# Modulation vectors of layer 1: one-row-per-condition matmuls replaced by weight-tile products on ACT, sums on GpSimd and one-column matmuls

## The chip, the cores and the metric

The kernel runs on 1 core of one Trainium2 chip. A core has five engines with a queue each, worked off in order: TensorE (PE, with its weight loads shown apart as PEld), VectorE (DVE), ScalarE (ACT), GpSimd (POOL) and SyncE (SP), which only issues transfers here. The metric is the device time of one execution in microseconds (us); the time shown is the median of three runs.

## What is computed

Two layers of a diffusion backbone over 512 latent tokens and 256 context tokens, model width 1024. Each layer's six modulation vectors (shift, scale and gate of the mixer, shift, scale and gate of the MLP) come from the condition `c`, and for the context from `c_ctx`:

```python
def adaln_modulation(cond, w_mod, b_mod):
    m = jax.nn.silu(cond) @ w_mod + b_mod          # w_mod: 1024 x 6144, one per layer
    return jnp.split(m[..., None, :], N_MOD, axis=-1)

for layer in range(DEPTH):                         # DEPTH = 2
    with_ctx_out = layer < DEPTH - 1
    sh1, sc1, g1, sh2, sc2, g2 = adaln_modulation(c, w_mod[layer], b_mod[layer])
    csh1, csc1, cg1, csh2, csc2, cg2 = adaln_modulation(c_ctx, w_mod[layer], b_mod[layer])
    h = rmsnorm(x, norm1_g[layer]) * (1.0 + sc1) + sh1
    h_c = rmsnorm(ctx, norm1_g[layer]) * (1.0 + csc1) + csh1
    mix, mix_c = hybrid_mixer(h, h_c, ...)         # S5 scan, gated DeltaNet, windowed attention, merge
    x = x + g1 * mix
    x = x + g2 * sq_relu_mlp(rmsnorm(x, norm2_g[layer]) * (1.0 + sc2) + sh2, w_ff1[layer], w_ff2[layer])
    if with_ctx_out:
        ...                                        # the same two updates of ctx, with cg1, csh2, csc2, cg2
return rmsnorm(x, final_norm_g)
```

In layer 1 the context has no output, so of its six vectors only `csh1` and `csc1` are used there: columns 0 to 2047 of the 6144.

## The kernel before

Everything is fp32. Features lie on the 128 partitions, tokens on the free axis; `x` is 128 x 8 x 768. A large product (`mm3`, L178) is three matmuls for each 128 x 128 weight tile: the weight and the activation are each split into a high part and a remainder, and high x high, high x low and low x high are added up in PSUM. `load_w` brings 128 x 1024 of weights (512 KB) over SP into `ws` (3 buffers), ACT writes the high part `wh` (L227), and the engine `g.wle` writes the remainder `wl` (L228): DVE in the MLP, GpSimd in most of the mixers. `wh` and `wl` have 2 buffers each, so ACT may start the split of a tile when PE has let go of the last but one.

The order of a run is: setup and modulation of layer 0, mixers, merge and MLP of layer 0, mixers, merge and MLP of layer 1. The change lies in the MLP of layer 0 (`mlp`, L1682 on). It works in four groups `gi`; each has eight up-projections (`up`, one weight tile column block `j` each, 24 matmuls of 512 columns and 24 of 256), relu and square, the split of the result (ACT `hh`, DVE `hl`), and then eight down-projections (`ff2`), whose results DVE adds to `x` (L1657). Between the up-projections, two background jobs that layer 1 needs are taken a step further, one step at a time:

- `adaln` (L241), the modulation of layer 1. One step is one block `nb` of 512 of the 6144 columns; there are 12, one after each odd `j`, so that the last comes in the third group. A step loads four tiles `wa` of 128 x 1024 (SP, 2 buffers), multiplies each half with the condition (`g.cs`, 32 columns of which two are used: row 0 is `c`, row 1 is `c_ctx`) as the stationary operand, eight fp32 matmuls of 512 columns, four of which stand side by side in the array's 32-column strips (L251); ACT copies the sums with a factor 0.5 (`ms`, L254), PE transposes them (L257), DVE adds the four strips (L259) and the bias (L261) into `g.modv`. Its two PSUM tiles come from the tag `s`, which has 2 buffers and serves the other background job too.
- `s5_tables` (L498 on), the tables of the S5 scan of layer 1. Sixteen steps, one after each `j`. Each is about fifty short DVE operations, transposes on PE (L558), small matmuls (L568) and DMAs of the results (L550, L561, L585). Its tiles `tX` and `tC` have one buffer each.

Layer 0's own modulation also uses `adaln`. A second call, `adaln(g, l + 1, ...)` in the MLP of layer 1, makes a generator that is never advanced. What layer 1 needs of `modv` is first read after the MLP (`norm_gain`, L275).

An engine's order is set when the program is built: the framework takes the instructions in program order as priority and simulates a timeline, and puts next on an engine what is ready in it. On the chip each engine then works off that fixed order and waits where a semaphore asks for it.

Of the kernel before, what the change touches and what calls it, by code (L numbers as in the profile page):

```python
# [8 lines left out]
F32 = mybir.dt.float32  # L9
# [3 lines left out]
OP = mybir.AluOpType  # L13
# [20 lines left out]
SM_G1, SM_G2, SM_GF, SM_BM, SM_CV, SM_DG, SM_SK, SM_AL, SM_DT, SM_D = 0, 16, 32, 40, 136, 256, 258, 274, 290, 306  # L34
# [120 lines left out]
def raw(t, off, dims):  # L155
    return bass.AP(tensor=t.tensor, offset=t.offset + off, ap=[list(t.ap[0])] + [list(x) for x in dims])
# [25 lines left out]
def setup(g):  # L182
    tc, nc, A = g.tc, g.nc, g.A
    es = g.es
    g.base = es.enter_context(tc.tile_pool(name="base", bufs=1))
    g.wp = es.enter_context(tc.tile_pool(name="wp", bufs=2))
    g.ps = es.enter_context(tc.tile_pool(name="ps", bufs=1, space=PSUM))
    g.dr = es.enter_context(tc.tile_pool(name="dr", bufs=1, space=DRAM))
    g.ca = g.base.tile([128, CA_N], F32, name="ca")
    nc.sync.dma_start(g.ca, A["ca"])  # L190
    g.sm = g.base.tile([128, SM_N], F32, name="sm")
    nc.sync.dma_start(g.sm, A["small"])
    g.ident = g.ca[:, CA_ID:CA_ID + 128]
    g.ones = g.base.tile([128, 32], F32, name="ones")
    nc.gpsimd.memset(g.ones, 1.0)
    g.cneg = g.base.tile([128, 1], F32, name="cneg")
    nc.gpsimd.memset(g.cneg, -0.5)
    g.cpos = g.base.tile([128, 1], F32, name="cpos")
    nc.gpsimd.memset(g.cpos, 0.5)
    g.hpi = g.base.tile([128, 1], F32, name="hpi")  # L200
    nc.gpsimd.memset(g.hpi, math.pi / 2)
    g.modv = g.base.tile([128, NL, 48, 2], F32, name="modv")
    g.g1 = g.base.tile([128, 8, 2], F32, name="g1a")
    g.g2 = g.base.tile([128, 8, 2], F32, name="g2a")

# [4 lines left out]
def pm(g, tag="m"):  # L210
    return g.ps.tile([128, 512], F32, name="p" + tag, tag=tag, bufs=PSB[tag])
# [9 lines left out]
def load_w(g, l, i, pool=None):  # L221
    nc = g.nc
    s = load_raw(g, g.A["wt"][l, i])
    pool, bufs = (g.wp, 2) if pool is None else (pool, 6)
    hi = pool.tile([128, 1024], F32R, name="wh", tag="wh", bufs=bufs)
    lo = pool.tile([128, 1024], F32R, name="wl", tag="wl", bufs=bufs)
    nc.scalar.copy(hi, s)  # L227
    g.wle.tensor_tensor(lo, s, hi.bitcast(F32), op=OP.subtract)  # L228
    return hi, lo
# [11 lines left out]
def adaln(g, l, nbs, pool, bufs=2):  # L241
    nc = g.nc
    for nb in nbs:
        ps = pm(g, "s")
        for kp in range(4):
            w = pool.tile([128, 1024], F32, name="wa", tag="wa", bufs=bufs)
            g.ad_last = nc.sync.dma_start(w, g.A["wmod"][l, nb, kp])
            for k2 in range(2):
                kt = kp * 2 + k2
                c = kt % 4  # L250
                nc.tensor.matmul(ps[32 * c:32 * c + 32, :], lhsT=g.cs[:, kt, :], rhs=w[:, k2 * 512:k2 * 512 + 512],  # L251
                                 start=kt < 4, stop=kt >= 4, tile_position=(0, 32 * c))
        ms = pool.tile([128, 512], F32, name="ms", tag="ms", bufs=1)
        nc.scalar.mul(ms, ps, 0.5)  # L254
        p2 = pm(g, "s")
        for j in range(4):
            nc.tensor.transpose(p2[:, j * 128:j * 128 + 128], ms[:, j * 128:j * 128 + 128], g.ident)  # L257
        md = pool.tile([128, 4, 2], F32, name="md", tag="md", bufs=1)
        nc.vector.tensor_reduce(md, raw(p2, 0, [[128, 4], [1, 2], [32, 4]]), axis=AX.X, op=OP.add)  # L259
        bm = g.sm[:, SM_BM + 48 * l + nb * 4:SM_BM + 48 * l + nb * 4 + 4]  # L260
        nc.vector.tensor_tensor(g.modv[:, l, nb * 4:nb * 4 + 4, :], md,  # L261
                                bm[:, :, None].to_broadcast([128, 4, 2]), op=OP.add)
        yield


def drain(it, n=1):
    for _ in range(n):
        next(it, None)
# [59 lines left out]
def passes(cx):  # L328
    return P_LC if cx else P_AB


def groups(cx):
    return [[p] for p in P_LC] if cx else [P_AB]
# [24 lines left out]
def gemm_x(g, w, grp, kts=range(8), src=None):  # L358
    ps = pm(g, "g")
    o = 0  # L360
    for p in grp:
        if src is None:
            hi, lo = g.hv[p.key]
            f = (lambda k: hi[:, k, :], lambda k: lo[:, k, :])
        else:
            f = (lambda k: src[k][0][:, p.sl], lambda k: src[k][1][:, p.sl])
        mm3(g, ps[:, o:o + p.n], w, list(kts), f)
        o += p.n
    return ps[:, :o], slice(grp[0].sl.start, grp[0].sl.start + o)
# [901 lines left out]
def split(g, hi, lo, src, scale):  # L1271
    g.nc.scalar.mul(hi, src, scale)
    g.nc.vector.scalar_tensor_tensor(lo, src, scale, hi.bitcast(F32), op0=OP.mult, op1=OP.subtract)
# [381 lines left out]
def ff2(g, l, w, m, p, hid):  # L1655
    acc, sl = gemm_x(g, w, [p], src=hid)
    g.nc.vector.scalar_tensor_tensor(g.x[:, m, sl], acc, g.modv[:, l, 40 + m, p.r:p.r + 1], g.x[:, m, sl],  # L1657
                                     op0=OP.mult, op1=OP.add)
# [23 lines left out]
def mlp(g, l, out):  # L1682
    nc, tc = g.nc, g.tc
    cx = l < NL - 1
    outs = ["l", "c"] if cx else ["l"]
    nn = TOK if cx else LAT
    if cx:
        tb = s5_tables(g, l + 1, lambda k, d: nc.vector, 1)
    with tc.tile_pool(name=f"ml{l}", bufs=1, reuse_waits="tile") as pool:
        ad = adaln(g, l + 1, range(12), pool)  # L1690
        def up(js, grps):
            ws = [load_w(g, l, W_F1 + j) for j in js]
            rs = [pool.tile([128, nn], F32, name="rl", tag="rl", bufs=2) for _ in js]
            for grp in grps:
                for w, r in zip(ws, rs):
                    acc, sl = gemm_x(g, w, grp)
                    nc.scalar.activation(r[:, sl], acc, AF.Relu)
            for r in rs:
                nc.vector.tensor_tensor(r, r, r, op=OP.mult)
                hh = pool.tile([128, nn], F32R, name="hh", tag="hh", bufs=9)  # L1700
                hl = pool.tile([128, nn], F32R, name="hl", tag="hl", bufs=9)
                split(g, hh, hl, r, 1.0)
                hid.append((hh, hl))

        for gi in range(4):
            hid = []
            for j in range(8):
                if gi > 0 or j > 1:
                    up([8 * gi + j], groups(cx))
                elif j == 0:  # L1710
                    up([0, 1], [[p] for p in passes(cx)])
                if cx:
                    drain(ad, j % 2)
                    drain(tb)
            last = gi == 3 and not cx
            if last:
                g.mp_.__exit__(None, None, None)
                last_group(g, l, pool, hid, out)
                break
            sts = [Stats(g, pool, p.n, 2, ("rl", nn), "ms") for p in P_LC] if cx and gi == 3 else None  # L1720
            ws = {}
            order = [(m, p) for m in range(8) for p in (P_LC if cx else P_LC[:1])]
            if sts:
                order = order[:12] + [(m, p) for p in P_LC for m in (6, 7)]
            for m, p in order:
                if m not in ws:
                    ws[m] = load_w(g, l, W_F2 + 8 * gi + m)
                ff2(g, l, ws[m], m, p, hid)
                if sts:
                    sts[P_LC.index(p)].add(m, g.x[:, m, p.sl])  # L1730
                    if m == 7:
                        st = sts[P_LC.index(p)]
                        g.pbs.append(st.bcast())
                        if PF and p.key == "l":
                            st.pace(PF)
                        else:
                            g.plan = []
    if cx:
        g.mp_.__exit__(None, None, None)
# [3 lines left out]
def hybrid_block(ctx, tc, A, out):  # L1743
# [3 lines left out]
    g.tb, g.hd, g.rside, g.pbs, g.plan, g.ldp, g.hst = {}, {}, "right", [], [], [], []  # L1747
    g.wle = nc.vector
    setup(g)
    s5a_open(g, 0)  # L1750
    cond_setup(g)
# [76 lines left out]
```

## Time and profile before

| | us |
|---|---|
| three runs | 2945.82, 2945.91, 2971.23 |
| median | 2945.91 |
| the profiled execution, its time | 2966.88 |
| the profiled execution, its span | 2965.1 |
| PE busy of the span | 2729.9 (92%) |
| DVE busy | 1669.2 (56%) |
| ACT busy | 908.1 (31%) |
| POOL busy | 558.1 (19%) |

Busy times are of the profiled execution. Matmuls overlap in the array, so PE's busy share is the share of time in which at least one runs, and the distance between the starts of two neighbours says what one costs. The MLP of layer 0 lies from about 1140 to 1765 us of the span. An fp32 matmul shows as two records (two LDWEIGHTS and two MATMUL), a transpose as one.

### The profile page before, as it was taken

The numbers are of one execution on the slowest core, as the hardware profiler recorded it, in microseconds if no ns is written. First come the engines' busy times: TensorE is split into PE (matmuls) and PEld (weight loads), VectorE is DVE, ScalarE is ACT, GpSimd is POOL, SyncE is SP. The second block draws the span as 40 slices with busy tenths as digits, with TensorE's granted clock in tenths as the row PEclk, the third lists the DMA queues.
The fourth block names the chain that finished last, engine by engine and source line by source line (L and its number), as shares of the span: only waits on it lengthen the run. The fifth ranks groups of instructions, "written<-read, shape, count | busy, mean of one in ns | idle before, by whom it ended". The sixth has DMA issues, their size and how long they took to land. (4 is left out here: it accounts for less than half of the span.)

```text
span 2965.1 us, 46215 instructions
## 1 busy us (share of the span) xinstructions
PE 2729.9 (92%) x17908; PEld 2193.9 (74%) x17908; DVE 1669.2 (56%) x4335; ACT 908.1 (31%) x1643; POOL 558.1 (19%) x733
## 2 busy tenths in 40 slices
PE   5698899999999999999999999758997999999998
PEld 1585578878677877787778878646775768789997
DVE  7839985245336647747432324997456368444443
ACT  2243344232222323223121324332342234323322
POOL 4643331030213300000000001442253133000000
PEclk8799899699999999999999999879997999999999
DMA  6564322236116433535341225223432226233231
GB/s 226 160 219 161 136 80 79 69 123 174 42 38 204 137 109 108 161 125 151 120 133 67 67 84 176 73 66 120 138 102 76 93 84 208 77 99 99 87 100 65
DMA packets 206620, 343.63 MB, mean 116 GB/s; under 512 B 89280, under 2 KB 121152, under 8 KB 206400
## 3 DMA queue, kind: packets, MB, share of 16 engines
q1 hardware_dynamic: 171712, 297.56, 31.4%
q0 software_dynamic: 9600, 36.71, 3.7%
q10 hardware_dynamic: 25088, 6.40, 1.0%
q8 instruction: 141, 2.31, 0.3%
q14 instruction: 79, 0.65, 0.1%
HBM read 269.04 MB, written 68.16 MB: 114 GB/s over the span
## 5 line engine op out<-in xcount | busy, mean ns | idle before, releaser
L228 DVE TENSOR_TENSOR wl<-ws,wh 128x1024 fp32r<-128x1024 f32 x234 | 293.5, 1256 | 341.0 <-ACT wh L227 306.8
L227 ACT CAST wh<-ws 128x1024 fp32r<-128x1024 f32 x272 | 284.8, 1049 | 606.4 <-PE pg L178 477.9
L178 PE MATMUL pg<-hhil,wh 128*128 128x512 f32 x720 | 296.4, 412 | 51.5 <-ACT cxp L867 35.9
L178 PE MATMUL pg<-hlol,wh 128*128 128x512 f32 x720 | 294.0, 409 | 0.4 <-DVE hlol L350 0.4
L178 PE MATMUL pg<-hhil,wl 128*128 128x512 f32 x720 | 293.1, 407 | 0.1
L178 PE MATMUL pg<-hh,wh 128*128 128x512 f32 (+1 forms) x832 | 285.6, 344 | 3.1 <-DVE x L1657 2.8
L178 PE MATMUL pg<-hlo,wh 128*128 128x512 f32 (+1 forms) x800 | 280.9, 351 | 6.2 <-DVE hlo L350 6.2
L178 PE MATMUL pg<-hhi,wh 128*128 128x512 f32 (+1 forms) x800 | 281.4, 352 | 5.1 <-ACT cxp L867 5.1
L178 PE MATMUL pg<-hh,wl 128*128 128x512 f32 (+1 forms) x832 | 284.0, 342 | 1.0 <-DVE wl L228 1.0
L178 PE MATMUL pg<-hl,wh 128*128 128x512 f32 (+1 forms) x832 | 284.7, 343 | 0.0
L178 PE MATMUL pg<-hhi,wl 128*128 128x512 f32 (+1 forms) x800 | 279.4, 349 | 0.0
L178 PEld LDWEIGHTS pg<-hhil,wh 128*128 128x128 f32 x720 | 139.5, 194 | 96.7 <-ACT cxp L867 37.4
L1657 DVE SCALAR_TENSOR_TENSOR x<-pg,modv,x 128x512 f32<-128x512 f32 (+1 forms) x104 | 64.9, 626 | 259.5 <-PE pg L178 259.3
L178 PEld LDWEIGHTS pg<-hlo,wh 128*128 128x128 f32 x800 | 154.7, 193 | 37.4 <-issue 14.0
L178 PEld LDWEIGHTS pg<-hh,wh 128*128 128x128 f32 x832 | 157.3, 189 | 33.8 <-issue 12.1
L178 PEld LDWEIGHTS pg<-hhi,wh 128*128 128x128 f32 x800 | 155.2, 194 | 31.6 <-issue 9.0
L178 PEld LDWEIGHTS pg<-hl,wh 128*128 128x128 f32 x832 | 157.4, 189 | 27.9 <-issue 10.6
L178 PEld LDWEIGHTS pg<-hhi,wl 128*128 128x128 f32 x800 | 154.6, 193 | 29.3 <-issue 11.7
L178 PEld LDWEIGHTS pg<-hh,wl 128*128 128x128 f32 x832 | 157.3, 189 | 22.8 <-issue 2.9
L178 PEld LDWEIGHTS pg<-hlol,wh 128*128 128x128 f32 x720 | 139.4, 194 | 36.8 <-issue 6.6
L178 PEld LDWEIGHTS pg<-hhil,wl 128*128 128x128 f32 x720 | 139.2, 193 | 36.9 <-issue 5.6
L307 POOL TENSOR_TENSOR nr<-nv,cneg 128x2 f32<-128x2 f32 (+1 forms) x10 | 9.3, 933 | 645.5 <-ACT nsq L290 350.2
(421 smaller groups left out, 6115.8 us busy)
## 6 DMA issues: line engine op xcount, KB each, us to landing
ws<-in_wt SPq DMA_DIRECT2D x272, 512.0 KB, 3.6
wa<-in_wmod SPq DMA_DIRECT2D x96, 512.0 KB, 4.3
gtd<-gr POOLq DMA_DIRECT2D x24, 384.0 KB, 2.9
tg<-gtd POOLq DMA_DIRECT2D x24, 384.0 KB, 3.5
tb<-tC SPq DMA_DIRECT2D x64, 128.0 KB, 2.3
cvd<-ctp SPq DMA_DIRECT2D x20, 384.0 KB, 2.6
gtd<-gr POOLq DMA_DIRECT2D x24, 256.0 KB, 2.6
tg<-gtd POOLq DMA_DIRECT2D x24, 256.0 KB, 3.1
```

Source lines behind the costliest of these rows:

```text
L178: g.nc.tensor.matmul(ps, lhsT=wt[:, a], rhs=x(k), start=i == 0, stop=i == n - 1)
L227: nc.scalar.copy(hi, s)
L228: g.wle.tensor_tensor(lo, s, hi.bitcast(F32), op=OP.subtract)
L307: nc.gpsimd.tensor_tensor(r[:, :m], v[:, :m], g.cneg.to_broadcast([128, m]), op=OP.pow)
L1657: g.nc.vector.scalar_tensor_tensor(g.x[:, m, sl], acc, g.modv[:, l, 40 + m, p.r:p.r + 1], g.x[:, m, sl], op0=OP.mult, op1=OP.add)
```

## The change

`adaln` stays for layer 0. For layer 1 a new generator `adaln_sums` does the 12 blocks. The same 48 tiles `wa` are loaded. For each of the eight 128-row pieces of a block, ACT multiplies the 128 x 512 weights by the condition, one value for each partition; the first product goes into an accumulator `as`, the others into `at` (2 buffers), and GpSimd adds them to the accumulator. Blocks 0 to 3 do it for both conditions (`nr` = 2), blocks 4 to 11 for `c` alone. Then PE sums over the partitions: the accumulator is the stationary operand, 128 columns at a time, against one column of 0.5 (`g.cpos`), four matmuls for a condition. DVE adds the bias. The context's column of `modv` is set to zero at the start, and the generator that was never advanced is no longer made in layer 1.

```diff
@@ setup
     g.modv = g.base.tile([128, NL, 48, 2], F32, name="modv")
+    nc.gpsimd.memset(g.modv[:, 1, :, 1], 0.0)
@@ after adaln
+def adaln_sums(g, l, nbs, pool):
+    nc = g.nc
+    for nb in nbs:
+        nr = 2 if nb < 4 else 1
+        acc = [pool.tile([128, 512], F32, name=f"as{r}", tag=f"as{r}", bufs=1) for r in range(nr)]
+        for kp in range(4):
+            w = pool.tile([128, 1024], F32, name="wa", tag="wa", bufs=2)
+            nc.sync.dma_start(w, g.A["wmod"][l, nb, kp])
+            for k2 in range(2):
+                kt = kp * 2 + k2
+                wk = w[:, k2 * 512:k2 * 512 + 512]
+                for r in range(nr):
+                    c = g.cs[:, kt, r:r + 1]
+                    if kt == 0:
+                        nc.scalar.mul(acc[r], wk, c)
+                    else:
+                        t = pool.tile([128, 512], F32, name="at", tag="at", bufs=2)
+                        nc.scalar.mul(t, wk, c)
+                        nc.gpsimd.tensor_tensor(acc[r], acc[r], t, op=OP.add)
+        ps = pm(g, "s")
+        for j in range(4):
+            for r in range(nr):
+                nc.tensor.matmul(ps[:, nr * j + r:nr * j + r + 1], lhsT=acc[r][:, 128 * j:128 * j + 128], rhs=g.cpos, start=True, stop=True)
+        bm = g.sm[:, SM_BM + 48 * l + nb * 4:SM_BM + 48 * l + nb * 4 + 4]
+        nc.vector.tensor_tensor(g.modv[:, l, nb * 4:nb * 4 + 4, :nr], ps[:, :4 * nr].rearrange("p (j r) -> p j r", j=4),
+                                bm[:, :, None].to_broadcast([128, 4, nr]), op=OP.add)
+        yield
@@ mlp
-        ad = adaln(g, l + 1, range(12), pool)
+        if cx:
+            ad = adaln_sums(g, l + 1, range(12), pool)
```

## Rows read from the trace of the kernel before

**Rows 1.** The page, span in 40 slices: busy tenths of PE.
```profile
PE   5698899999999999999999999758997999999998
```
**Rows 2.** Windows: PE, PEld, DVE, ACT, POOL busy; TensorE clock, DMA share, GB/s.
```profile
1150.00:1290.00 140.00, 140.00 (x810) 109.43 (x809) 103.66 (x484) 37.77 (x64) 0.00 (x0) 1.00 0.52 146
1290.00:1440.00 150.00, 149.64 (x854) 117.68 (x854) 95.03 (x418) 37.70 (x65) 0.00 (x0) 1.00 0.47 144
1440.00:1565.00 125.00, 125.00 (x698) 97.45 (x697) 37.62 (x50) 30.79 (x44) 0.00 (x0) 1.00 0.35 116
...
1820.00:1980.00 160.00, 119.72 (x741) 98.71 (x739) 135.78 (x319) 63.97 (x119) 66.25 (x62) 0.87 0.27 91
```
**Rows 3.** Groups by line, 1130 to 1765 us: busy us, mean ns, idle before.
```profile
L228 DVE TENSOR_TENSOR wl<-ws,wh 128x1024 fp32r<-128x1024 f32 x62 | 75.8, 1223 | 129.3 <-ACT wh L227 99.9 <-PE ps L251 29.3
...
L227 ACT CAST wh<-ws 128x1024 fp32r<-128x1024 f32 x62 | 64.9, 1047 | 183.3 <-PE pg L178 180.5 <-DVE tux L523 1.9 <-ACT thx L576 0.9
...
L251 PE MATMUL ps<-wa,conds 128*32 128x512 f32 x192 | 42.6, 604 | 0.1
...
L257 PE MATMUL ps<-ca,ms 128*128 128x128 f32 x48 | 7.2, 272 | 0.0
```
**Rows 4.** Timeline of PE around one batch of modulation matmuls: start, length, records.
```profile
1187.99 0.28 PE L178 MATMUL pg<-hhic,wl 128*128 128x256 f32 x1
1188.19 1.06 PE L251 MATMUL ps<-wa,conds 128*32 128x512 f32 x8
1189.19 0.38 PE L178 MATMUL pg<-hhic,wh 128*128 128x256 f32 x1
```
**Rows 5.** Timeline of PE around the four transposes of one block.
```profile
1203.21 0.40 PE L178 MATMUL pg<-hhil,wh 128*128 128x512 f32 x1
1203.45 0.40 PE L178 MATMUL pg<-hlol,wh 128*128 128x512 f32 x1
1203.69 0.60 PE L257 MATMUL ps<-ca,ms 128*128 128x128 f32 x4
1204.12 0.60 PE L558 MATMUL ps<-ca,tX 128*128 128x128 f32 x4
```
**Rows 6.** Timeline of PE around four one-column fp32 matmuls of the statistics.
```profile
1766.67 0.28 PE L178 MATMUL pg<-hl,wh 128*128 128x256 f32 x1
1766.79 0.28 PE L178 MATMUL pg<-hh,wl 128*128 128x256 f32 x1
1766.96 1.05 PE L302 MATMUL pm<-ca,ms 128*128 128x1 f32 x8
1767.87 0.36 PE L178 MATMUL pg<-hh,wh 128*128 128x256 f32 x1
```
**Rows 7.** Timeline of PE around two such matmuls, another place.
```profile
1139.57 0.39 PE L178 MATMUL pg<-hlol,wh 128*128 128x512 f32 x1
1139.80 0.50 PE L302 MATMUL pm<-ca,nrow 128*128 128x1 f32 x4
1140.16 0.48 PE L178 MATMUL pg<-hhil,wl 128*128 128x512 f32 x1
```
**Rows 8.** Groups by line and shape, whole span: GpSimd add and ACT product of 128x512.
```profile
L880 POOL TENSOR_TENSOR cac<-cac,ctp 128x512 f32<-128x512 f32 x8 | 11.0, 1381 | 10.9 <-DVE cac L876 7.3 <-ACT ctp L879 3.6
...
L879 ACT ACTIVATE ctp<-cxp,sm 128x512 f32<-128x512 f32 x8 | 5.7, 717 | 4.6 <-POOL cac L880 2.3 <-DMA cvd<-ctp 1.7 <-POOL cxp L866 0.6
```
**Rows 9.** Timeline of DVE and POOL in the mixers of layer 1.
```profile
1964.94 0.26 DVE L653 TENSOR_TENSOR rt<-st,A 128x64 f32<-128x64 f32 x1
...
1965.78 1.35 POOL L880 TENSOR_TENSOR cac<-cac,ctp 128x512 f32<-128x512 f32 x1 [0.73 <-ACT ctp L879]
1965.94 1.27 DVE L653 TENSOR_TENSOR rt<-st,A 128x64 f32<-128x64 f32 x1
```
**Rows 10.** Waits, whole span: who waited for whom, total us, times, longest.
```profile
ACT cxp L881 <- POOL cac L880: 46.0, 18, 6.7
```
**Rows 11.** Waits of PE from 1820 to 1980 us, same columns.
```profile
PE pg L178 <- ACT cxp L867: 37.8, 6, 11.5
```

## The prediction

> **What bounds the kernel now.** I read the page's slices first: PE is at nine tenths or more from slice 16 to slice 24, the MLP of layer 0 [rows 1]. Then the windows of that stage: from 1150 to 1565 us PE is busy all the time (140.00 of 140, 149.64 of 150, 125.00 of 125), at full granted clock, GpSimd does nothing, ACT is busy 106 of 415 us, and DVE is the second busiest: 104 of 140 us in the first stretch, 95 of 150 in the second, 38 of 125 in the third [rows 2]. The first two are loaded because the tables of layer 1 are made there. Then the groups by line, to see what of PE is the modulation: 192 records on L251 and 48 on L257 [rows 3]. Last, the timeline around single batches, for what one costs PE in distance between starts. The stage is bound by PE, so PE time taken out of it comes off the kernel's time, as long as no other engine becomes late.
>
> **PE: what goes.** Four modulation matmuls side by side (8 records) put the next product 1189.19 - 1187.99 = 1.20 us after the one before, where a 256-column product alone takes 0.12 (1766.67 to 1766.79): 1.08 us a batch, busy 1.06 [rows 4, 6]. L251 is busy 42.6 us in all, which is 42.6 / 1.06 = 40 batches, more than the 24 that 12 blocks would need, because a block's tiles come in pairs and so its matmuls in parts [rows 3, 4]. 40 x 1.08 = 43.4 us. Four transposes cost 1204.12 - 1203.45 - 0.24 = 0.43 us (0.24 is the step of a 512-column product), times 12 is 5.2 us [rows 5]. Removed: 48.6 us.
>
> **PE: what comes.** 4 x 8 + 8 x 4 = 64 one-column fp32 matmuls. The trace has the same form on L302: four cost 1767.87 - 1766.79 - 0.12 = 0.96 us, 0.24 each [rows 6]; in another place two cost 0.59 - 0.23 = 0.36, 0.18 each [rows 7]. So 11.5 to 15.4 us; I take 15.4, since the groups here are of four and eight. A column costs almost what a whole 128-column weight load costs, so these are not free. Net for PE: 48.6 - 15.4 = 33.2 us gained (up to 37). The gain falls evenly enough: about 8 us of it in the first stretch, where blocks 0 to 3 with two conditions need 32 of the 64 columns' matmuls.
>
> **ACT.** 4 blocks x 16 + 8 x 8 = 128 products, 0.717 us each by the tap product of the same shape [rows 8]: 92 us. With the 106 us there that is 198 of 415 us, under half. By sum it is no bound. ACT also makes `wh` (1.05 us), and DVE `wl` (1.22 us) behind it [rows 3]; a weight tile lasts PE 24 x 0.24 + 24 x 0.12 = 8.6 us, so a tile's split may be about 8.6 - 2.3 = 6.3 us late before PE waits. Cost: nothing, while that cover holds.
>
> **GpSimd.** 4 x 14 + 8 x 7 = 112 adds at 1.38 us [rows 8]: 155 us, of which 77 in blocks 0 to 3, 39 in blocks 4 to 7, 39 in blocks 8 to 11. GpSimd is free here [rows 2]. A block with two conditions needs 14 x 1.38 = 19.3 us in a chain, one with one condition 9.7 us; `at` has two buffers, so ACT runs at GpSimd's pace.
>
> **What GpSimd does to DVE.** This is the term on which the sign hangs. In the mixers of layer 1, a DVE operation on two SBUF operands that takes 0.26 us took 1.27 when a GpSimd add of the same shape as the new ones ran from 1965.78 to 1967.13: it started 0.16 us later and ended with it [rows 9]. So an add keeps such an operation waiting until it is over, and a dense chain lets DVE make about one of them per add, where it makes 484 / 140 = 3.5 operations a us now [rows 2]. The Trainium skill says this as a rule (SBUF — State Buffer, section "SBUF: two separate sides"): DVE and GpSimd share one pair of ports, whoever starts first holds it for the whole instruction, and DVE needs it with two SBUF inputs. By that rule, too, the two engines' times would be added up here.
>
> If nothing of DVE overlaps an add, the first stretch needs 104 + 77 = 181 us on the two together, and PE would now need 140 - 8 = 132: 49 us too much. The second needs 95 + 39 = 134 of about 138, the third 38 + 39 = 77 of about 112: both fit [rows 2, 8]. So the upper bound of the sum is 49 us, the lower one nothing: over the whole of 1150 to 1565 us DVE has 415 - 236 = 179 us idle, more than the 155 us of adds, and chains that fall into it cost nothing. The nearest row is the mixers of layer 1, where the two engines meet in the same way: from 1820 to 1980 us GpSimd is busy 66 us, DVE 136, and PE stands idle 160 - 119.7 = 40 us, 0.61 us for each us of GpSimd [rows 2], almost all of it (37.8 us, 6 times) waiting for one copy on ACT [rows 11]. 0.61 x 77 = 47 us. That stretch has other chains in it as well, and DVE is fuller. I take 40 us, and none for blocks 4 to 11. How it reaches PE: `wl`, and the tables' `tX` and `tC`, stand on DVE behind held operations; PE's order is fixed, its transposes of the tables and its products with `wl` stand in front of everything else.
>
> **The rest, at no cost.** The 48 tiles `wa` are loaded as before; SP waits for their buffers on ACT's products in place of PE's matmuls. On SP the weights `ws` stand behind them, with three buffers and the 6.3 us of above as cover. DVE loses the reduction over strips and keeps the bias add. One memset of 48 values at the start and a generator that never ran are nothing. Each block holds one PSUM tile of tag `s` for a moment, where before it held two in turn; this helps the tables, which use the same two buffers.
>
> **Sum.** -33.2 + 40 = +7 us. Against the profiled execution's 2966.9 us that is 2974; I put it on the median, 2945.9, which lies 21 us below the profiled time: 2953 us. The stretch was at full clock in the profile, so I carry the differences over unscaled.
>
> **Rivals.**
>
> *The gain stays.* The chains fall into DVE's idle time, or the order on PE leaves enough room. For it: 179 us idle against 155 us of adds, and the 6.3 us cover. Against it: the chain of a two-condition block is dense and lies in the fullest stretch. Loss 0 to 4: 2945.9 - 33.2 to -37 = 2909 to 2917 us.
>
> *Slower: PE waits in its queue at the column matmuls.* They stand in PE's fixed order, and all products behind them wait if GpSimd's last add is late; nothing fills that. The mechanism is seen on ACT: its tanh behind a chain of GpSimd adds waited 46.0 us in 18 times, 2.6 us on average, 6.7 at the longest [rows 10]. 12 blocks x 2.6 = 31 us on top of the 40: 2945.9 + 7 + 31 = 2984 us; at 6.7 us each it would be 80 more, 3033. It decides against the change alone when a block's wait passes 33.2 / 12 = 2.8 us. Against it: a block's columns have a long way to their place where the tables and the weights come between, and the accumulator, which has one buffer, is free again right after.
>
> *It does not do what it says.* Should other work on PE just move into the freed time while the end stays bound by something else, the time would stay at 2946 us. Against it: PE without gaps up to 1565 us [rows 2]. It falls within the forecast's range.
>
> **How the numbers follow.** Forecast, a net change between -25 and +29 us: 0.53, with 2921 to 2975 as its own range. The gain stays: 0.17. Slower: 0.30. About 1%, 29 us, is what a measurement of this kernel can tell from no change: its three runs lie 25 us apart. So faster by over 1% (below 2916) has 0.17, within 1% 0.53, slower by over 1% 0.30. The range leaves out under one in ten at each side: from 2914, near the full gain, to 2995, beyond the 2984 of the second rival.
>
> **What the profile after would show.** Step by step: PE's records of the modulation in layer 0's MLP gone and 64 one-column matmuls of about 0.24 us in their place; ACT's products at about 0.72 us and GpSimd's adds at 1.38 us or, where they wait for DVE, more; DVE's table operations and `wl` with maxima of 1.3 to 2.6 us in place of 0.27 and 1.22; idle time of PE, now next to nothing between 1150 and 1565 us, of some 40 us, put down to DVE `wl`, `tX` or `tC`, most of it at blocks 0 to 3. If that idle time is put down to GpSimd's adds at the column matmuls, the second rival was right. If PE has no gaps and the MLP of layer 0 is some 33 us shorter, the first was, and my price of the sharing was wrong. The prediction would also be wrong if the order on the engines comes out quite different from before, since then the stretches of DVE's load above don't hold.

## The result, and the profile after

| | before | after |
|---|---|---|
| median of four runs each, us | 2955.1 | 2992.6 |
| lowest and highest, us | 2945.8, 2971.2 | 2981.5, 2996.7 |
| profiled execution, time and span, us | 2966.9, 2965.1 | 2981.5, 2979.7 |

The kernel became slower: ratio 1.010, 95% interval 1.0054 to 1.0146, or 16 to 43 us; the medians lie 37.5 us apart. The forecast, 2953 us, was 39.6 us too low. The result lies above the forecast's own range (2921 to 2975), in the class "slower" that had a chance of 0.30, and inside the widest range (2914 to 2995) by 2.4 us.

The windows of the profile after, same columns as [rows 2]. The first three answer to the first three of [rows 2]; the other four are 10-us windows of the same stage.

```profile
1150.00:1290.00 140.00, 120.59 (x622) 99.42 (x621) 130.40 (x416) 65.59 (x108) 73.62 (x50) 0.86 0.46 138
1290.00:1440.00 150.00, 136.99 (x758) 113.36 (x758) 120.54 (x429) 55.71 (x94) 41.55 (x29) 0.96 0.48 144
1440.00:1565.00 125.00, 125.00 (x730) 109.47 (x729) 43.86 (x48) 42.44 (x61) 30.21 (x21) 1.00 0.32 107
...
1190.00:1200.00 10.00, 10.00 (x48) 8.79 (x48) 9.70 (x30) 4.87 (x9) 4.48 (x3) 0.56 0.69 210
...
1220.00:1230.00 10.00, 7.79 (x49) 6.73 (x48) 9.88 (x30) 4.00 (x6) 4.64 (x3) 0.97 0.32 79
1230.00:1240.00 10.00, 10.00 (x36) 7.85 (x35) 7.42 (x31) 5.67 (x11) 2.61 (x3) 0.52 0.65 214
...
1330.00:1340.00 10.00, 10.00 (x57) 8.42 (x56) 3.05 (x3) 2.93 (x5) 0.00 (x0) 1.00 0.18 63
```

Two things happened in the first two stretches. PE, which had next to no gap before (0.36 us in the second), is idle 19.4 and 13.0 us. And its granted clock, 1.00 before, is 0.86 and 0.96. From 1230 to 1240 it is 0.52, nearly the lower of the two levels (1.2 of 2.4 GHz), although PE is busy all ten of the ten microseconds; in the ten before, PE had stood idle for 2.2. In 1330 to 1340, where GpSimd does nothing, the clock is full.

What PE waited for, in the waits of PE from 1100 to 1800 us of the profile after (total us, times, longest):

```profile
PE ps L598 <- DVE tC L554: 7.9, 4, 3.5
PE pg L178 <- DVE x L1687: 7.2, 4, 4.7
PE pg L178 <- DVE wl L229: 6.0, 1, 6.0
PE ps L588 <- DVE tX L554: 5.1, 3, 3.0
PE pg L178 <- ACT rl L1728: 3.6, 3, 2.2
...
PE ps L289 <- POOL as L285: 1.2, 1, 1.2
```

The four largest are waits on DVE, and 33.6 of the 43.0 us in all are; but for one of 6.0 us they come in pieces of up to 4.7. The wait on GpSimd's last add at the column matmuls is one of 1.2 us.

The new work, in the groups by line and shape (columns as in [rows 3]):

```profile
L285 POOL TENSOR_TENSOR as<-as,at 128x512 f32<-128x512 f32 x112 | 166.2, 1494 | 267.3 <-ACT as L281 195.5 <-ACT at L284 69.3
...
L284 ACT ACTIVATE at<-wa,conds 128x512 f32<-128x512 f32 x112 | 78.8, 719 | 88.1 <-DMA wa<-in_wmod 22.3 <-DVE tuc L553 20.2 <-POOL as L285 17.3
...
L289 PE MATMUL ps<-cpos,as 128*128 128x1 f32 x128 | 18.5, 258 | 1.2 <-POOL as L285 1.2
```

What GpSimd did to DVE is seen in the mean time (ns) of DVE's table operations, groups of DVE from 1125 to 1440 us. Before:

```profile
L228 DVE TENSOR_TENSOR wl<-ws,wh 128x1024 fp32r<-128x1024 f32 x28 | 34.1, 1219 | 31.9 <-ACT wh L227 26.4 <-PE ps L251 5.6
L523 DVE TENSOR_TENSOR tux<-tB,apw 128x112 f32<-128x112 f32 x128 | 27.7, 267 | 0.2
...
L535 DVE COPY tz<-tB 64x32 f32<-64x32 f32 x64 | 11.1, 174 | 15.3 <-PE ps L568 14.7
...
L543 DVE TENSOR_SCALAR tcn<-tcc 128x32 f32<-128x32 f32 x32 | 5.5, 173 | 0.2
```

After, the same four:

```profile
L553 DVE TENSOR_TENSOR tux<-tB,apw 128x112 f32<-128x112 f32 x128 | 43.2, 385 | 0.2
L229 DVE TENSOR_TENSOR wl<-ws,wh 128x1024 fp32r<-128x1024 f32 x25 | 32.7, 1308 | 6.0 <-ACT wh L228 6.0
L565 DVE COPY tz<-tB 64x32 f32<-64x32 f32 x64 | 27.6, 431 | 9.4 <-PE ps L598 8.8
...
L573 DVE TENSOR_SCALAR tcn<-tcc 128x32 f32<-128x32 f32 x32 | 9.9, 309 | 0.1
```

The copy of a 64x32 tile takes 431 ns on the mean where it took 174.

**How the kernels are compared from here on.** Not by their spans: PE's granted clock between 400 and 700 us, in layer 0's mixers, differs from profile to profile with the same code. In the windows of before and of after:

```profile
400.00:700.00 300.00, 291.37 (x1938) 243.86 (x1937) 140.42 (x450) 108.84 (x254) 58.71 (x113) 0.90 0.31 99
```

```profile
400.00:700.00 300.00, 289.89 (x2036) 242.16 (x2037) 159.72 (x506) 111.83 (x259) 59.73 (x115) 0.98 0.33 107
```

So the MLP of layer 0 began at 1145.8 us in the one profile and at 1124.6 in the other. Over the eleven profiles of this study that clock lies between 0.89 and 0.98 and the start between 1122.7 and 1148.0. I therefore measure **the stage**: from the start of the first relu of layer 0's MLP to the first column matmul of its closing statistics (the one of [rows 6]). It is split into PE's idle time in it, and the time lost to the clock: in windows of 10 us, PE's busy time times one minus the granted clock, added up. The remainder is what the stage's work takes PE at full clock.

| kernel | stage | PE idle | lost to the clock | remainder |
|---|---|---|---|---|
| before | 621.2 | 1.0 | 0.0 | 620.2 |
| after | 654.0 | 40.0 | 23.0 | 591.0 |
| e1_memset | 612.8 | 17.4 | 8.3 | 587.1 |
| e2_noadd | 592.5 | 3.5 | 1.4 | 587.6 |
| e3_late | 605.0 | 9.4 | 5.8 | 589.8 |
| e4_before_late | 635.1 | 2.2 | 0.0 | 632.9 |
| e5_first4 | 616.7 | 16.4 | 5.3 | 595.0 |
| e6_late_held | 593.5 | 4.5 | 0.0 | 589.0 |
| e7_late_dve | 590.5 | 2.2 | 0.0 | 588.3 |
| e8_dve | 599.8 | 5.0 | 2.9 | 591.9 |
| e9_stalls | 639.5 | 32.9 | 14.4 | 592.2 |

The stage of after is 32.8 us longer than that of before: 29.2 us less work, 39.0 us more idle time, 23.0 us lost to the clock. The rest of the span behind it is 1198 to 1207 us in all eleven. Each stage is read from one profile; the differences of the stages from that of before agree with those of the medians below within 7.8 us.

### The profile page after: what moved, and what is told of

The parts are those of the page before. It is cut to its first block, busy times and chain, and to the rows that moved or that the text cites. A ratio compares the mean times of both kernels' runs of the same rounds, so it can differ in the third digit from the quotient of the medians.

```text
span 2979.7 us, 46296 instructions
## 1 busy us (share of the span) xinstructions
PE 2699.1 (91%) x17796; PEld 2194.0 (74%) x17796; DVE 1752.9 (59%) x4323; ACT 982.0 (33%) x1759; POOL 723.2 (24%) x846
## 5 line engine op out<-in xcount | busy, mean ns | idle before, releaser
L285 POOL TENSOR_TENSOR as<-as,at 128x512 f32<-128x512 f32 x112 | 166.2, 1494 | 267.3 <-ACT as L281 195.5
L178 PEld LDWEIGHTS pg<-hlo,wh 128*128 128x128 f32 x800 | 154.7, 193 | 37.7 <-issue 14.4
```

The lines of the kernel that those rows point to most:

```text
L178: g.nc.tensor.matmul(ps, lhsT=wt[:, a], rhs=x(k), start=i == 0, stop=i == n - 1)
L285: nc.gpsimd.tensor_tensor(acc[r], acc[r], t, op=OP.add)
```

## The experiments

### e2_noadd: the change without its adds

```diff
                         nc.scalar.mul(t, wk, c)
-                        nc.gpsimd.tensor_tensor(acc[r], acc[r], t, op=OP.add)
```

> Leaves out the GpSimd adds altogether: only the first product of each block reaches the column matmuls. ACT's 128 products and the 64 column matmuls stay. Theory (DVE held by GpSimd) and the rival of GpSimd's length both say 588 to 595 us for the MLP of layer 0, which is 621 less the 33 us of PE work saved. Third possibility (ACT's products delay the weight splits, or the new order of the instructions is what costs): the stage stays above 615 us.

Measured: 2942.0 us beside 2966.1 of before, ratio 0.9926 (0.9897 to 0.9954). The stage takes 592.5 us, 28.7 less than before and 61.5 less than after. The windows of e2_noadd:

```profile
1150.00:1290.00 140.00, 140.00 (x824) 117.18 (x823) 105.05 (x495) 70.39 (x118) 0.00 (x0) 1.00 0.60 179
1290.00:1440.00 150.00, 150.00 (x876) 127.58 (x875) 88.29 (x341) 60.23 (x97) 0.00 (x0) 1.00 0.48 148
```

PE has no gaps here and full clock, with the products on ACT and the column matmuls in place. So ACT's 128 products and the columns themselves hold next to nothing up (PE is idle 3.5 us in the whole stage), and the loss of 61.5 us comes with GpSimd's adds.

### e1_memset: GpSimd as busy, but reading nothing

```diff
-                        t = pool.tile([128, 512], F32, name="at", tag="at", bufs=2)
-                        nc.scalar.mul(t, wk, c)
-                        nc.gpsimd.tensor_tensor(acc[r], acc[r], t, op=OP.add)
+                        t = pool.tile([128, 1536], F32, name="at", tag="at", bufs=2)
+                        nc.scalar.mul(t[:, :512], wk, c)
+                        if kt < 7:
+                            nc.gpsimd.memset(t, 0.0)
+                        else:
+                            nc.gpsimd.memset(t[:, :1024], 0.0)
+                            nc.gpsimd.memset(acc[r], 0.0)
```

> Leaves out the sums: in place of each GpSimd add of 128x512 a GpSimd memset of about the same length (1536 columns, some 1.4 us by the memsets in the trace) on the product's tile, which reads nothing from SBUF; ACT's products, the tile waits and the column matmuls stay. Measure: the MLP of layer 0 from its first relu to the first column matmul of its closing statistics, 621 us before, 654 us after. Theory (the adds' SBUF reads hold DVE's two-operand operations): DVE's operations stay at 0.27 and 1.22 us, PE has under 10 us of gaps, its clock stays at full, the stage takes 588 to 597 us and the kernel is about 1% faster than before. Rival (it is GpSimd's length: the column matmuls and ACT wait for a chain of 10 to 19 us): the chain is as long as with the adds, so the stage stays at 640 to 655 us.

Measured: 2958.0 us beside 2966.1, ratio 0.9968 (0.9943 to 0.9993); the stage 612.8 us. Memsets, which read no tile, cost 20.3 of the adds' 61.5 us: a third, neither nothing nor all. The stage misses both the theory's interval (588 to 597) and the rival's (640 to 655). Which DVE operations they still hold is seen in the groups of DVE of e1_memset from 1125 to 1440 us:

```profile
L569 DVE COPY tz<-tB 64x32 f32<-64x32 f32 x64 | 39.6, 618 | 7.0 <-PE ps L602 6.3
L229 DVE TENSOR_TENSOR wl<-ws,wh 128x1024 fp32r<-128x1024 f32 x27 | 33.1, 1228 | 7.7 <-ACT wh L228 7.6
L577 DVE TENSOR_SCALAR tcn<-tcc 128x32 f32<-128x32 f32 x32 | 20.4, 639 | 0.0
L557 DVE TENSOR_TENSOR tuc<-tcc,apw 128x128 f32<-128x128 f32 x64 | 16.3, 296 | 0.1
```

and singly in its timeline, first DVE, then GpSimd (start, length):

```profile
1168.45 0.49 DVE L557 TENSOR_TENSOR tuc<-tcc,apw 128x128 f32<-128x128 f32 x2
1168.86 0.48 DVE L557 TENSOR_TENSOR tuc<-tcn,apw 128x128 f32<-128x128 f32 x2
...
1169.43 1.16 DVE L571 COPY tX<-tB 128x32 f32<-128x32 f32 x1
1169.52 1.07 DVE L465 TENSOR_TENSOR cm<-tbb,sf 128x16 f32<-128x16 f32 x1
...
1167.85 4.08 POOL L286 MEMSET at<- 128x1536 f32 x3
```

The products `tuc`, with two SBUF operands, keep 0.49 us for two while a memset runs. The copy that comes next takes 1.16 us where the same copy takes 0.18 free of GpSimd, and what is queued behind it ends only with it. In the means, copies go to 618 ns and the operation with a constant to 639, while `wl` and `tuc` stay at 1228 and 296. Other operations with two operands do rise, `tux` from 267 to 537 ns, but only behind a held one: of the DVE operations from 1125 to 1440 us that took over 0.12 us longer than before and didn't just stand behind such a one, all 51 are copies or operations with a constant, and each ends with a memset. In after there are 78, held 1.04 us each on the mean, and 46 of them have two operands. The Trainium skill (SBUF — State Buffer, section "SBUF: two separate sides") has this finer rule: a DVE operation with two SBUF inputs needs the shared ports only against a GpSimd operation that reads SBUF, while one in a two-port mode needs them against any. The trace agrees on the first half, and on the second if the copies and the operation with a constant run in such a mode, which no row names. My prediction had named only the first half.

### e8_dve: the sums on DVE itself, at the change's own places

```diff
-                        nc.scalar.mul(acc[r], wk, c)
+                        nc.vector.tensor_scalar(acc[r], wk, c, None, op0=OP.mult)
                     else:
-                        t = pool.tile([128, 512], F32, name="at", tag="at", bufs=2)
-                        nc.scalar.mul(t, wk, c)
-                        nc.gpsimd.tensor_tensor(acc[r], acc[r], t, op=OP.add)
+                        nc.vector.scalar_tensor_tensor(acc[r], wk, c, acc[r], op0=OP.mult, op1=OP.add)
```

> The change with product and sum in one VectorE operation, at the places of the change: all blocks as early as there, no ACT and no GpSimd. VectorE gets about 45 us more in the first stretch, where it is busy 111 of 150 us before, and 22 in the second (94 of 150). Theory, what costs is that GpSimd holds VectorE's small operations for a whole add at a time: VectorE's own work of 0.75 us a piece delays less, the stage takes 598 to 615 us, and VectorE's copies of the tables keep their 0.17 to 0.20 us. Rival, VectorE is simply too full beside the tables, whichever engine takes its time: 111 + 45 = 156 us in a stretch of 140, and the stage takes 625 to 655 us.

Measured: 2952.7 us beside 2966.3, ratio 0.9945 (0.9913 to 0.9976); the stage 599.8 us. In a window and in the groups of DVE of e8_dve:

```profile
1150.00:1290.00 140.00, 135.78 (x786) 113.51 (x785) 136.17 (x506) 35.49 (x62) 0.00 (x0) 0.98 0.53 153
```

```profile
L283 DVE SCALAR_TENSOR_TENSOR as<-wa,conds,as 128x512 f32<-128x512 f32 x112 | 82.8, 749 | 6.4 <-DMA wa<-in_wmod 5.7
...
L563 DVE COPY tz<-tB 64x32 f32<-64x32 f32 x64 | 11.1, 173 | 3.4 <-PE ps L596 2.7
```

DVE carries 90 us more of its own work, is busy 136 of 140 us beside the tables, and yet PE loses 4.2 us there instead of 19.4. The tables' copies take 173 ns. So the loss of after isn't that DVE was too full; it is that GpSimd held it, for about a microsecond at a time, in front of short operations for which PE waits. The rival of this run falls.

### e3_late and e4_before_late: the blocks moved behind the tables

```diff
-                    drain(ad, j % 2)
+                    drain(ad, gi > 1)
```

The same edit in after (e3_late) and in before (e4_before_late).

> The whole change, but the twelve blocks stand after the up-projections of groups three and four (one per step), where the tables are done and DVE is about 30% busy. Theory (DVE held by GpSimd): there DVE has room for all 155 us of adds, PE's gaps stay under 10 us, the stage takes 588 to 605 us and the kernel is 0.5 to 1.1% faster than before. Rival (column matmuls wait in PE's queue for a late chain): blocks come faster there, one per 8.6 us of PE against chains of 10 to 19 us, so waits of 2 to 10 us for each of twelve blocks, 620 to 680 us.

> The kernel before, with its modulation blocks moved to groups three and four in the same way. Theory: PE sets the stage and its work is the same, so 621 us within 6 and the kernel within 0.3% of before. Rival (the place of the blocks alone, by the PSUM buffers shared with the tables and by the order, is worth something): more than 6 us either way; then the comparison of the late version has to be made against this one.

Measured: e3_late 2946.7 us, ratio to before 0.9945 (0.9917 to 0.9973), stage 605.0; e4_before_late 2981.5 us, ratio 1.0057 (1.0035 to 1.0079), stage 635.1. The same method that loses 33 us at its places wins 16 at later ones. It isn't the place as such: the old method loses 14 us by the same move, where about the same time was expected. So at the late places the new method is to be held against e4_before_late, and its stage is 30.1 us shorter. The groups of e4_before_late show part of what the move costs the old method:

```profile
L251 PE MATMUL ps<-wa,conds 128*32 128x512 f32 x192 | 47.4, 605 | 0.0
```

against 42.6 in [rows 3]: the same 192 records stand less side by side. By the distances between starts, a group of four records (two matmuls) costs PE 0.98 us and one of eight (four matmuls) 1.00; of the groups 37 have four records and 2 have eight, where before has 24 and 6.

### e6_late_held: no block beside the tables at all

```diff
-            nc.sync.dma_start(w, g.A["wmod"][l, nb, kp])
+            with g.tc.issue_after(g.wl_last):
+                nc.sync.dma_start(w, g.A["wmod"][l, nb, kp])
```

on top of e3_late, in which 28 adds still ran before 1441 us.

> The whole change with the blocks drained only in groups three and four of the MLP, as in e3_late, and the loads of the modulation's weight tiles issued only after the latest load of a product's weights, so that block 0 can't start early: in e3_late 28 adds still ran beside the tables. Theory, the 12.5 us by which e3_late's stage (605.0 us) lies above that without adds (592.5) come from those 28 adds: the stage takes 592 to 599 us, and VectorE's copies and small operations of the tables take 0.17 to 0.21 us again. Rival, they come from the moved blocks themselves, as moving cost 14 us in the kernel before: the stage stays at 603 to 612 us.

Measured: 2943.6 us beside 2966.3, ratio 0.9908 (0.9871 to 0.9945); the stage 593.5 us. One window of e6_late_held:

```profile
1440.00:1565.00 125.00, 122.72 (x722) 107.98 (x722) 52.48 (x50) 71.68 (x105) 90.94 (x63) 1.00 0.52 167
```

GpSimd is busier here than anywhere in after, 91 of 125 us, and PE loses 2.3 us. DVE is busy 52 of 125: it has few short operations to be held, and room to make up for it. The 12.5 us that e3_late's stage lay above e2_noadd's are down to 1.0, so they were those 28 adds, of which 22 ran beside the tables. Here the first add starts 30 us after the last DVE operation of the tables, and the tables' copies take 173 ns.

### e7_late_dve: the same places, on DVE

The edits of e8_dve on top of e6_late_held.

> As e6_late_held, but product and sum in one VectorE operation (weight tile times condition plus accumulator), 112 of them and 16 plain products, and neither ACT nor GpSimd takes part. Estimate of one: 0.75 us, that of the nearest operation on VectorE, the one with two tensors and a scalar at 128x512; 112 x 0.75 + 16 x 0.4 = 90 us on VectorE, which is busy 94 of 321 us in the last two stretches of the stage before. Theory, GpSimd is what costs, and VectorE has room there: the stage takes 590 to 602 us. Rival, the products stand in front of the split of the weights on VectorE and make it late: over 610 us, with idle time of TensorE put down to the low half of the weights.

Measured: 2929.3 us beside 2966.3, ratio 0.9866 (0.9817 to 0.9915), the fastest of all; the stage 590.5 us. PE is idle 2.2 us in it, 1.0 in before, and its clock is full. It is 30.7 us shorter than before's, the gain that the change was worth on PE. e6_late_held comes within 3.0 us of it in the stage. In these two the other work of the stage stands in nearly the same order (1000 of 1002 instructions on DVE, 3230 of 3234 on PE), so the 3.0 us, of one profile each, are about what ACT and GpSimd cost there.

### e5_first4: blocks 0 to 3 by the old batches

```diff
-            ad = adaln_sums(g, l + 1, range(12), pool)
+            ad = iter(list_chain(adaln(g, l + 1, range(4), pool), adaln_sums(g, l + 1, range(4, 12), pool)))
```

`list_chain` runs one generator after the other.

> Blocks 0 to 3 (two conditions) are made by the batches of four matmuls as before, blocks 4 to 11 by products on ACT, adds on GpSimd and columns. 56 of the 112 adds go, the ones that stood in the first stretch beside the tables' densest work on VectorE. The stage is the time from the first relu of layer 0's MLP to the first column matmul of its closing statistics: 621.2 us before, 654.0 after, 592.5 without any add. Theory, the adds of blocks 0 to 3 cause most of the loss of 61.5 us: the gain of TensorE for eight blocks is 8 x (28.7 + 12.8)/12 - 32 x 0.20 = 21 us, blocks 4 to 11 lose the 12 us of idle time seen for them after, and the stage takes 608 to 616 us. Rival, each add costs the same wherever it stands: 31 us of loss stay, 621 - 21 + 31 = 631 us, 625 to 637.

Measured: 2961.7 us beside 2966.3, ratio 1.0002 (0.9974 to 1.0031); the stage 616.7 us, a little over the theory's interval and far from the rival's. Its windows:

```profile
1150.00:1290.00 140.00, 139.03 (x800) 108.78 (x797) 110.09 (x488) 42.97 (x71) 9.29 (x7) 1.00 0.57 166
1290.00:1440.00 150.00, 135.34 (x759) 112.27 (x758) 116.79 (x400) 55.93 (x95) 40.19 (x28) 0.95 0.47 140
```

The first stretch is whole again; the second is as in after (idle 14.7 and 13.0 us, clock 0.95 and 0.96). So 40 us of adds in that second stretch cost about 15 us of idle time and some clock, though DVE and GpSimd together had room there by sum. Of the 39.0 us that PE stands idle more in after than in before, 15.4 remain here: they belong to blocks 4 to 11, and 23.6 to blocks 0 to 3.

### e9_stalls: what lowers the clock

On top of e7_late_dve, where no clock is lost, eight waits are put into PE's queue:

```diff
...
+                if cx and gi > 1 and j % 2:
+                    sx = pool.tile([128, 512], F32, name="sx", tag="sx", bufs=1)
+                    nc.scalar.mul(sx, hid[-1][0].bitcast(F32)[:, :512], 1.0)
+                    g.stall = nc.tensor.matmul(pm(g, "s")[:, :1], lhsT=sx[:, :128], rhs=g.cpos, start=True, stop=True).ins
...
-                    acc, sl = gemm_x(g, w, grp)
+                    with tc.issue_after(g.stall) if g.stall else nullcontext():
+                        acc, sl = gemm_x(g, w, grp)
```

> As e7_late_dve, in which GpSimd and ACT take no part in the modulation and TensorE kept full clock in the whole stage, with eight waits put into TensorE's queue in groups three and four: after every second up tile one more one-column matmul, whose result nobody uses, needs a copy on ACT of the tile just squared, and the products of the next up tile stand behind it. Work added elsewhere: eight 0.72 us copies on ACT. For six of the eight nothing else stands between, so TensorE is expected idle for the relu, the square (1.22 us), the high half (about 1 us) and the copy, 3 to 4 us each, 18 to 24 us in all; before them the idle time of the stage was 2 us. It tells what lowers TensorE's clock in the kernel after, where 40 us of idle time came with about 23 us of lost clock. Theory, the waits of TensorE themselves: 10-us windows behind the waits show 0.5 to 0.9, about half a us is lost for each us of idle time, and the stage takes 590.5 + 21 + 10 = 622 us (615 to 630). Rival, something else of that kernel (GpSimd's activity, the load of VectorE, traffic): the clock stays at 1.00 and the stage takes 590.5 + 21 = 612 us (607 to 614).

Measured: 2989.0 us beside 2969.7, ratio 1.0073 (1.0047 to 1.0098); the stage 639.5 us, above both the theory's interval (615 to 630) and the rival's (607 to 614). PE's waits, three of its windows, and PE around one wait in the timeline of e9_stalls:

```profile
PE ps L1747 <- ACT sx L1746: 22.6, 5, 6.2
PE ps L288 <- DVE as L284: 7.8, 4, 5.6
```

```profile
1480.00:1490.00 10.00, 9.43 (x57) 8.06 (x55) 9.87 (x15) 3.99 (x6) 0.00 (x0) 1.00 0.65 207
1490.00:1500.00 10.00, 7.96 (x31) 6.63 (x31) 9.23 (x15) 1.59 (x3) 0.00 (x0) 0.66 0.60 185
1500.00:1510.00 10.00, 10.00 (x64) 8.94 (x64) 6.70 (x10) 2.77 (x4) 0.00 (x0) 1.00 0.54 175
```

```profile
1488.59 0.28 PE L178 MATMUL pg<-hhic,wl 128*128 128x256 f32 x1
1489.23 0.35 PE L288 MATMUL ps<-cpos,as 128*128 128x1 f32 x2 [0.36 <-DVE as L284]
1489.80 1.72 PE L288 MATMUL ps<-cpos,as 128*128 128x1 f32 x14 [0.22 <-DVE as L284]
1493.56 0.58 PE L1747 MATMUL ps<-cpos,sx 128*128 128x1 f32 x2 [2.04 <-ACT sx L1746]
1494.00 0.77 PE L178 MATMUL pg<-hhil,wh 128*128 128x512 f32 x1
...
1497.13 0.63 PE L178 MATMUL pg<-hlol,wh 128*128 128x512 f32 x1
1497.56 0.63 PE L178 MATMUL pg<-hhil,wl 128*128 128x512 f32 x1
```

Behind a wait of 2.04 us, and column matmuls and small gaps before it, the 512-column products follow each other in 0.43 us instead of 0.23, and then, from 1499.60 on, in 0.23 again. GpSimd does nothing in this stretch. The idle time rose by 30.7 us over that of e7_late_dve, more than the 18 to 24 expected, because the blocks' own column matmuls now wait as well (7.8 us). The time lost to the clock rose by 14.4: 0.47 us for each us of idle time, where half was expected. Waits of PE are enough to lower the clock without GpSimd; the rival, by which it stays at 1.00, falls. Nor do GpSimd and DVE lower it by being busy. A window of e1_memset, in which PE has no gap:

```profile
1268.10:1278.10 10.00, 10.00 (x59) 8.62 (x58) 9.85 (x46) 6.14 (x10) 7.83 (x7) 1.00 0.83 263
```

In after the ratio is 23.0 / 39.0 = 0.59, and in the table the loss follows the idle time roughly: over that of before, 0.34 (e5_first4) to 0.69 (e3_late) us are lost for each us where the idle time is over 8 us, while nothing is lost at 2.2 and 4.5 us of it but 1.4 at 3.5 and 2.9 at 5.0.

## Why the prediction was right or wrong

**PE's gain: right, a little large.** 33.2 us were predicted. The remainders give 29.2 for after and 31 to 32 for e6_late_held and e7_late_dve. The columns cost 0.20 us each at full clock, between the two bounds (0.18, 0.24). The batches were priced too high: the distances between starts add up to 38.3 us for the records on L251 in the stage before (188 of the 192), where 40 times the one distance read made 43.4.

**ACT at no cost: right.** 0.719 us a product as priced, and e2_noadd shows 3.5 us of gaps in PE with all of them in place. In after, where ACT runs at GpSimd's pace, 1.9 us of PE's waits are put down to a product.

**GpSimd's adds: right as to their size when free.** The median is 1.31 us, near the 1.38 priced; the mean is 1.49 and the longest 3.24, which began together with a DVE operation of 0.95 us. 166 us in place of 155.

**GpSimd holding DVE: the right mechanism, and the sign hung on it as said.** PE's idle time, 40 us, was predicted to the microsecond, put down to `wl`, `tX` and `tC` among others. But the figure is right by luck, by two errors. For blocks 0 to 3 it was 23.6 us, not 40: 0.3 us for each of the 77 us of adds, half of the rate taken from the mixers. That rate came from a stretch in which PE waited for a copy on ACT [rows 11], so it was no price of this mechanism. For blocks 4 to 11, priced at nothing, it was 15.4. The test used there, that DVE's and GpSimd's busy times add up to less than the stretch, failed: a short operation that is late by one add makes PE late by that much at once, even where DVE has time to spare afterwards. It holds only where DVE has little for PE to wait for, as in e6_late_held.

**The missing term.** The differences were carried over unscaled, since the stage was at full clock. That step failed. A stage that gets 39.0 us of gaps doesn't keep its clock: 23.0 us went there, and e9_stalls shows that waits do it without GpSimd. With the measured terms the sum is -29.2 + 39.0 + 23.0 = +32.8 us instead of +7. Of the 39.6 us by which the forecast missed, that is 25.8. Another 9 lie in the base: before has 2955 us by four runs, 9 more than by the three shown. The rest, about 5 us, is within the spread of the runs; beside the experiments, 26 and 25 runs of before have medians of 2966.1 and 2966.3 us, so the stage is the surer measure.

**The rivals.** PE waiting at the column matmuls for GpSimd: 1.2 us in all, against 31 priced; the chains were done before their columns' turn, as the argument against it said. The time came out near that rival's, 2984, for another reason. The range reached to 2995 because of this rival, so that it held the result is luck too. The gain that stays: it does, in e7_late_dve, when GpSimd is left out and the work is put behind the tables; not in after.

**The order on the engines.** The prediction named it as a way to be wrong, and no run with the blocks at their early places holds it fixed: of about 1000 DVE operations in the stage that don't belong to the modulation, 776 come in the same order in before and after, and 782 in e2_noadd and after. What speaks against the order as the cause is that it differs as much between kernels that keep PE's idle time at 5.0 us or less (755 between before and e2_noadd, 738 between before and e8_dve).

**Still open**: why the move costs the old method 12.7 us of PE work, of which 4.8 are seen in the busy time of its batches; and how much of after's loss the changed order carries.

## What to carry to other kernels

Work that is taken off the busiest engine is not free because its new engine is idle: ask which engine the new one holds up, and what short operations of that one the busiest engine waits for; price the delay of each, not the sum of busy times. Where GpSimd would run beside a dense chain of DVE, either put its work into a stretch where DVE has little to do, or give the whole of it to DVE, even a nearly full DVE: 0.75 us there replaced 0.72 on ACT plus 1.31 to 1.49 on GpSimd. And where TensorE will wait for many microseconds in a stage at full clock, add about half a microsecond for the clock to each: 0.34 to 0.69 in these runs, 0.47 where the waits were put in without GpSimd.

## What the runs showed of the hardware that was not expected

- GpSimd memsets, which read nothing, hold DVE's copies and operations with a constant (174 to 618 ns, 173 to 639 ns on the mean), though not its two-operand operations themselves (282 to 296, 1219 to 1228), which are late only behind a held one.
- A batch of two fp32 matmuls side by side costs PE 0.98 us, one of four 1.00 (e4_before_late).
- Waits of PE of a few microseconds, 2.04 in one place, are followed by products at nearly half the pace (0.43 for 0.23 us) in a stage that otherwise keeps full clock.
- PE's granted clock in a stage of the same code differs between profiles (0.89 to 0.98 from 400 to 700 us), and shifts all that follows by up to 25 us.
